# Down weights' sums on GpSimd, last norms and flips reordered, seven low parts made by accumulating DMAs

## The chip, the cores and the metric

The kernel runs on one core of a Trainium2 chip. Its time is the device time of one launch in microseconds (us). Five engines work side by side, each through its own queue of instructions in order: TensorE (PE, matmuls), VectorE (DVE), ScalarE (ACT), GpSimd (POOL) and SyncE (SP, which issues the loads here). DMAs run beside them. Engines wait for each other by semaphores.

## What is computed

One layer of a decoder trunk for 512 tokens of width 1024, in float32: attention with forget gates, a projection and a norm, a gated MLP with a short causal convolution (2816 channels), a second norm, and an embedding that is projected and gated into the result.

```python
mix = fox_mixer(x, attn_w_in, attn_b_f, attn_w_out)
x = layer_norm(ALPHA * x + mix, ln_mix_g, ln_mix_b)
u, g = jnp.split(x @ ffn_w_up, [FFN_DIM], axis=-1)
g = causal_dwconv(g, ffn_conv_w, ffn_conv_b)
ffn = (jax.nn.gelu(g, approximate=False) * u) @ ffn_w_down
x = layer_norm(ALPHA * x + ffn, ln_ffn_g, ln_ffn_b)
gate = jax.nn.sigmoid(x @ ple_w_gate + ple_b_gate)
out = x + gate * (p @ ple_w_proj)
```

## The kernel before

**Every product is three matmuls.** A float32 operand is cut into a high part (rounded to fp32r) and a low part (the rest); hi x hi, hi x lo and lo x hi are added in PSUM (`three`, L107).

**Weights arrive in units of 128 x 1024** (class `Weights`): a load from HBM into one of 4 `raw` buffers, ACT copies it to `whi` (L85), DVE takes `wlo = raw - whi` (L86), each into one of 5 buffers. `get(i, ahead)` hands out unit i and has the units up to i + ahead cut before it, so that the cutting instructions of the units ahead stand in the queues before the work on unit i.

**The stages** are: the input projections and attention (16 heads), with the output projection begun among the last heads; the norm of the mixer (L492, L494: two instructions for each 512 columns of a tile of 128 tokens); `up` with 22 pairs of gate and value tiles; `down` in two parts, behind 6 and behind 5 pairs of channel blocks; the second norm; the embedding product `pl` (L107, PSUM tiles `pl`); the gates `gt`; the output.

**`down` is a Strassen-Winograd product.** The halves of tokens, of channels and of output columns make blocks; seven block products replace eight. Four groups of units are worked one behind the other: `ua` (plain), `ub` (t12: two sums for a unit, L157 and L158, the second into the buffer `side`), `uc` (t3: one sum, L165), `ud` (t4: one sum with `side`, L172, of half size). The sums are over 128 x 512 weights, 4 for each of the 11 pairs, 44 in all, on DVE. The products go to six PSUM banks: x, y and z, two each. When a group ends, DVE adds its banks into the residual `y` (`give`, `add_half`, L476 and L478), and the next group's matmuls into that bank wait for it.

**The tail.** Behind part 1's `uc` the tiles of tokens 2 and 3 are complete, and `half_stats` and `norm` (L483 to L494, with one tiny POOL instruction, the power, L489) run for them; `ud` completes the tiles 0 and 1 one behind the other. `flip` (L502 to L507) transposes a normed tile on PE (`nt`), and ACT and DVE cut it into `x2h` and `x2l`, from which the gates are computed. The embedding products are seven of six matmuls and the four flips stand among them.

**The order** of each engine's instructions is made when the program is built: the scheduler keeps the code's order in the main, and lets an instruction pass another where its own cost figures say that it is ready earlier. So the code's order and each queue's differ by a few places. POOL does little but the attention's rescaling (L357, 64 instructions) and the eight powers.

Of the kernel before, what the change touches and what calls it, by code (L numbers as in the profile page):

```python
# [8 lines left out]
F32 = mybir.dt.float32  # L9
# [38 lines left out]
class Weights:  # L48
# [7 lines left out]

    def add(self, src, n=UNIT, inner=None, make=None):

        self.units.append((src, n, inner, make))
        return len(self.units) - 1  # L60

    def load_to(self, i):
        while self.loaded < min(i, len(self.units)):
            src, n, inner, make = self.units[self.loaded]
            t = self.pool.tile([P, UNIT], F32, tag="raw", name=f"raw{self.loaded}", bufs=RAW_BUFS)
            v = t[:, :n]
            if inner is not None:
                v = v.rearrange("p (a b) -> p a b", b=inner)
            self.nc.sync.dma_start(v, src)
            if make is not None:  # L70
                make(None)
            self.raw[self.loaded] = t
            self.loaded += 1

    def cut_to(self, i):
        while self.cut < min(i, len(self.units)):
            self.load_to(self.cut + 1)
            _, n, _, make = self.units[self.cut]
            t = self.raw.pop(self.cut)
# [3 lines left out]
            for piece in [t[:, :n]] if make is None else make(t):  # L83
                e = c + piece.shape[-1]
                self.nc.scalar.activation(hi[:, c:e], piece, AF.Copy)  # L85
                self.nc.vector.tensor_sub(lo[:, c:e], piece, hi[:, c:e].bitcast(F32))  # L86
                c = e
# [10 lines left out]
def trunk_layer(ctx: ExitStack, tc: tile.TileContext, xT, x2d, pT, wqk, wv0, wv1, wv2, bf, wo, wup, cwb,  # L98
# [46 lines left out]
    def down_units(part):  # L145
# [3 lines left out]
        def t12(j, i):  # L149
            def make(t):  # L150
# [5 lines left out]
                t1, t2 = t[:, :512], side[part][:, i, :]  # L156
                nc.vector.tensor_sub(t1, t1, t2)  # L157
                nc.vector.tensor_sub(t2, t[:, 512:], t1)  # L158
                return [t1, t2]
            return make  # L160

        def t3(t):
            if t is None:
                return None
            nc.vector.tensor_sub(t[:, :512], t[:, 512:], t[:, :512])  # L165
            return [t]

        def t4(i):
            def make(t):
                if t is None:  # L170
                    return None
                nc.vector.tensor_sub(t[:, :512], t[:, :512], side[part][:, i, :])  # L172
                return [t[:, :512]]
            return make
# [9 lines left out]
    for part in range(2):  # L184
        for f in range(2 * PAIRS[part][0], 2 * PAIRS[part][-1] + 2):
            u_up.append([W.add(wup[f, s], inner=P) for s in (1, 0)])
        u_dn.append(down_units(part))
    u_p = W.add(pT.rearrange("(k p) t -> p k t", p=P), inner=S)
    u_pl = [W.add(half_rows(wpl, 0, 2, n), inner=512) for n in range(2)]
    u_g = [[W.add(half_rows(wg, 2 * j, 2, n), inner=512) for j in range(4)] for n in range(2)]  # L190

# [293 lines left out]
    def norm(t, g, b):  # L485
# [3 lines left out]
        nc.gpsimd.tensor_tensor(mv[:, 3:4], mv[:, 2:3], neghalf, op=ALU.pow)  # L489
        for n in range(2):  # L490
            c = slice(n * 512, (n + 1) * 512)
            nc.vector.scalar_tensor_tensor(y[:, t, c], y[:, t, c], mv[:, 0:1], g[:, c],  # L492
                                           op0=ALU.subtract, op1=ALU.mult)
            nc.vector.scalar_tensor_tensor(y[:, t, c], y[:, t, c], mv[:, 3:4], b[:, c],  # L494
                                           op0=ALU.mult, op1=ALU.add)

# [76 lines left out]
    def down(part, hh, hl):  # L573
# [4 lines left out]
        A11, A22, A12, S1, S2, S3, S4 = range(7)  # L578
        acc = {(b, i): bank(f"{b}{part}{i}") for b in "xyz" for i in range(2)}
        seen, opened = set(), set()  # L580

        def step(b, i, a, u, col, first, last):

            j, u = u
            hi, lo = W.get(u)
            c, tk = slice(col * 512, col * 512 + 512), slice(a * HALF + i * P, a * HALF + (i + 1) * P)
# [4 lines left out]

        def chain(b, a, us, col, n):
            for i in range(2):
                step(b, i, a, us[n], col, n == 0, n == len(us) - 1)

# [26 lines left out]
        give("z", 0, 1)  # L622
        if part == 1:
            for t in (2, 3):
                for n in range(2):
                    half_stats(t, n)
                norm(t, g2, b2)
        us = list(enumerate(ud))
        for i in range(2):
            for n in range(len(js)):  # L630
                step("x", i, A22, us[n], 0, n == 0, n == len(js) - 1)
            give1("x", 1, 0, i)
            if part == 1:
                for n in range(2):
                    half_stats(i, n)
                norm(i, g2, b2)
                if i == 1:
                    flip(2, x2h, x2l)

# [33 lines left out]
    pl = base.tile([P, NT, D], F32, tag="xl", name="pl")  # L673
    W.cut_to(u_p + 3)

    def embed(ps, up, ul, p0, pw, lo_c=0, w=512):

        ph, plo = W.parts[up]
        hi, lo = W.get(ul)
        for k in range(2):  # L680
# [4 lines left out]
    for i, (n, t) in enumerate([(n, t) for n in range(2) for t in tiles][:-1]):  # L685
        ps = bank(f"pl{t}_{n}")
        embed(ps, u_p, u_pl[n], t * P, S)
        nc.scalar.activation(pl[:, t, n * 512:(n + 1) * 512], ps, AF.Copy)
        if i in (1, 3, 6):
            flip({1: 3, 3: 0, 6: 1}[i], x2h, x2l)  # L690

# [23 lines left out]
    for n in range(2):  # L715
        for t in tiles[:NT - n]:
            finish(n, t, gate(n, t), pl[:, t, n * 512:(n + 1) * 512])
    tz = tiles[-1]
# [53 lines left out]
```

## Time and profile before

| what | value |
|---|---|
| median of three runs | 677.21 us (676.69 to 678.17) |
| the profiled execution | 679.51 us |
| its span, first to last instruction | 677.8 us |
| mean granted TensorE clock | 0.986 |
| loads from HBM | 76.26 MB |

The trace is of one execution. A busy share is an average over stages, and where an engine is nearly always busy, what can be won lies in the few places where it is not. Those are found in three steps: the busy tenths over 40 slices of the span show where, the view of waits names which instruction waited and for whom, and the view of windows gives PE's busy time and granted clock in a stretch. The clock matters, since a matmul at a lower clock counts as busy all the same.

### The profile page before, as it was taken

The page shows a single profiled execution, that of the slowest core. Times are in us where ns is not written, and L with a number is a line of the kernel's source. Part 1 is how long each engine was busy: PE and PEld are TensorE (multiplying, and loading weights), DVE is VectorE, ACT ScalarE, POOL GpSimd, SP SyncE. Part 2 cuts the span into 40 slices and gives each one's busy share as a digit, 9 for nine tenths or more (in the row PEclk, how much of TensorE's full clock was granted, in tenths as well). Part 3 has the DMA queues.
Part 4 walks back from the last instruction along what each step waited for, and adds up shares of the span by engine and source line. Part 5 has one row for each costly group of instructions (what it writes and reads, how often), then busy time and mean ns, then how long its engine had stood idle before and what let it go on. Part 6 is the DMA issues. An engine that isn't in the chain of part 4 may idle for free.

```text
span 677.8 us, 8719 instructions
## 1 busy us (share of the span) xinstructions
PE 657.6 (97%) x3222; PEld 556.8 (82%) x3222; DVE 477.5 (70%) x762; ACT 314.9 (46%) x517; POOL 80.9 (12%) x78
## 2 busy tenths in 40 slices
PE   8999999999999999999999998999999999986997
PEld 7899888888888889888888886888888888765886
DVE  6664799999984895565556597565555669898454
ACT  5644687777774144344344343154344435243331
POOL 0000555544452110000000000000000000010000
PEclk9999999999999999999999998999999999996999
DMA  8533211221181314332233354572233327454321
GB/s 282 156 126 125 62 65 64 64 61 39 61 301 57 110 63 137 102 104 93 94 94 93 112 170 138 180 255 94 93 100 91 99 85 247 141 155 122 103 79 46
DMA packets 34011, 79.06 MB, mean 117 GB/s; under 512 B 3056, under 2 KB 6896, under 8 KB 33968
## 3 DMA queue, kind: packets, MB, share of 16 engines
q1 hardware_dynamic: 33968, 78.50, 36.0%
q8 instruction: 25, 0.41, 0.2%
q14 instruction: 18, 0.15, 0.1%
HBM read 76.26 MB, written 2.10 MB: 116 GB/s over the span
## 4 chain that ended last, share of the span: by engine, by line
PE 82%; DVE 8%; DMA 5%; issue 2%; ACT 2%; SPq 0%; ACTq 0%; DVEq 0%
PE g L107 17%; PE u L107 17%; PE pp L107 12%; PE gt L107 6%; PE pv L107 5%; PE x L107 5%; DMA raw<-wdn 4%; PE ao L107 3%; PE o L383 3%; DVE wlo L86 2%; PE t L370 2%; PE ap L107 2%; PE z L107 2%; PE pl L107 2%; PE s L339 1%
## 5 line engine op out<-in xcount | busy, mean ns | idle before, releaser
L86 DVE TENSOR_TENSOR wlo<-raw,whi 128x1024 fp32r<-128x1024 f32 (+4 forms) x138 | 149.4, 1089 | 80.2 <-ACT whi L85 79.7
L85 ACT ACTIVATE whi<-raw 128x1024 fp32r<-128x1024 f32 (+4 forms) x138 | 131.5, 956 | 158.1 <-PE g L107 51.9
L357 POOL TENSOR_SCALAR pr<-pr,rl 128x128 f32<-128x128 f32 (+1 forms) x64 | 72.8, 1157 | 134.9 <-DVE rl L353 132.7
L107 PE MATMUL g<-x1l,whi 128*128 128x512 f32 (+1 forms) x192 | 71.4, 372 | 1.2 <-DVE x1l L507 1.2
L107 PE MATMUL g<-x1h,whi 128*128 128x512 f32 (+1 forms) x192 | 71.4, 372 | 0.0
L107 PE MATMUL g<-x1h,wlo 128*128 128x512 f32 (+1 forms) x192 | 71.3, 371 | 0.0
L107 PE MATMUL u<-x1l,whi 128*128 128x512 f32 (+1 forms) x184 | 69.9, 380 | 0.0
L107 PE MATMUL u<-x1h,whi 128*128 128x512 f32 (+1 forms) x184 | 69.9, 380 | 0.0
L107 PE MATMUL u<-x1h,wlo 128*128 128x512 f32 (+1 forms) x184 | 69.9, 380 | 0.0
L489 POOL TENSOR_TENSOR mv<-mv,neghalf 128x1 f32<-128x1 f32 x8 | 7.3, 913 | 397.9 <-DVE mv L488 375.6
L107 PE MATMUL pp<-xh,wlo 128*128 128x512 f32 x128 | 50.2, 392 | 0.0
L107 PE MATMUL pp<-xl,whi 128*128 128x512 f32 x128 | 50.0, 391 | 0.0
L107 PE MATMUL pp<-xh,whi 128*128 128x512 f32 x128 | 49.9, 390 | 0.0
L107 PEld LDWEIGHTS g<-x1l,whi 128*128 128x128 f32 x192 | 36.2, 188 | 7.7 <-DVE x1l L507 1.4
L349 ACT ACTIVATE pr<-s,nm 128x128 f32<-128x128 f32 (+1 forms) x64 | 33.5, 526 | 16.8 <-DVE nm L348 15.8
L107 PEld LDWEIGHTS g<-x1h,wlo 128*128 128x128 f32 x192 | 36.2, 188 | 6.2
L107 PEld LDWEIGHTS g<-x1h,whi 128*128 128x128 f32 x192 | 36.1, 188 | 6.2
L107 PEld LDWEIGHTS u<-x1h,wlo 128*128 128x128 f32 x184 | 34.6, 188 | 6.6
L107 PEld LDWEIGHTS u<-x1h,whi 128*128 128x128 f32 x184 | 34.6, 188 | 6.5
L107 PEld LDWEIGHTS u<-x1l,whi 128*128 128x128 f32 x184 | 34.6, 188 | 6.5
L557 DVE TENSOR_TENSOR E<-a,u 128x512 f32<-128x512 f32 x22 | 15.1, 688 | 34.2 <-PE u L107 32.7
L556 ACT ACTIVATE a<-a 128x512 f32<-128x512 f32 x22 | 13.9, 632 | 52.6 <-DVE a L554 52.6
(156 smaller groups left out, 1430.5 us busy)
## 6 DMA issues: line engine op xcount, KB each, us to landing
raw<-wup SPq DMA_DIRECT2D x44, 512.0 KB
raw<-wdn SPq DMA_DIRECT2D x33, 512.0 KB
raw<-wqk SPq DMA_DIRECT2D x16, 512.0 KB
raw<-wo SPq DMA_DIRECT2D x8, 512.0 KB
raw<-wg SPq DMA_DIRECT2D x8, 512.0 KB
raw<-wv SPq DMA_DIRECT2D x8, 384.0 KB
side<-wdn SPq DMA_DIRECT2D x11, 256.0 KB
raw<-wdn SPq DMA_DIRECT2D x11, 256.0 KB
```

What stands on the lines that cost most here:

```text
L85: self.nc.scalar.activation(hi[:, c:e], piece, AF.Copy)
L86: self.nc.vector.tensor_sub(lo[:, c:e], piece, hi[:, c:e].bitcast(F32))
L107: nc.tensor.matmul(ps, lhsT, rhs, start=start and n == 0, stop=stop and n == 2, skip_group_check=on)
L339: nc.tensor.matmul(ps[:, :n], QA[:, q], KA[:, :n], start=True, stop=False)
L349: nc.scalar.activation(pr[:, off:off + w], ps[:, :w], AF.Exp, bias=nm[:, i:i + 1], accum_out=ls[:, i:i + 1])
L357: nc.gpsimd.tensor_scalar_mul(pr[:, off:off + w], pr[:, off:off + w], rl[:, i:i + 1])
L370: nc.tensor.transpose(ps[:, w:w + P], pr[:, o:o + P], ident)
L383: nc.tensor.matmul(ps[:, q0:], V[:, j, h], p[:, o:o + w], start=j == 0 and n == 0, stop=j == NT - 1 and n == 1)
L489: nc.gpsimd.tensor_tensor(mv[:, 3:4], mv[:, 2:3], neghalf, op=ALU.pow)
L556: nc.scalar.activation(a, a, AF.Gelu)
L557: nc.vector.tensor_mul(e, a, pu)
```

## The change

Six things are done at once.

- The 44 sums of the down weights are issued to GpSimd instead of DVE.
- Seven units (`pT`, the two of the embedding weights `wpl`, the first four of the gate weights `wg`) get their low part in another way (`by_dma`): ACT writes the negative of the weights, rounded to fp32r like `whi`, into `wlo` (L88 after), and a DMA that POOL issues adds the float32 weights from HBM to it (L90 after).
- A norm's two steps take 1024 columns in one instruction each instead of 512 in two (8 norms).
- `get` cuts 2 units ahead in the groups `ua`, `ub` and `uc`, and 3 in `ud` and in the embedding, instead of 1; the fixed cut of the three embedding units goes.
- In `ud` the loop runs over units outside and over the two banks inside. The norms of tiles 2 and 3 stand behind the matmuls of `ud`, those of tiles 0 and 1 behind the first gate.
- The flips: tile 2 behind the embedding products, tile 3 behind the first gate, then 0 and 1 each a gate later. The banks are allotted in the order y, z, x.

```diff
--- before.py
+++ after.py
@@ -54,14 +54,15 @@
         self.units, self.raw, self.parts = [], {}, {}
         self.loaded = self.cut = 0
 
-    def add(self, src, n=UNIT, inner=None, make=None):
-
-        self.units.append((src, n, inner, make))
+    def add(self, src, n=UNIT, inner=None, make=None, by_dma=False):
+
+
+        self.units.append((src, n, inner, make, by_dma))
         return len(self.units) - 1
 
     def load_to(self, i):
         while self.loaded < min(i, len(self.units)):
-            src, n, inner, make = self.units[self.loaded]
+            src, n, inner, make, _ = self.units[self.loaded]
             t = self.pool.tile([P, UNIT], F32, tag="raw", name=f"raw{self.loaded}", bufs=RAW_BUFS)
             v = t[:, :n]
             if inner is not None:
@@ -75,7 +76,7 @@
     def cut_to(self, i):
         while self.cut < min(i, len(self.units)):
             self.load_to(self.cut + 1)
-            _, n, _, make = self.units[self.cut]
+            src, n, inner, make, by_dma = self.units[self.cut]
             t = self.raw.pop(self.cut)
             hi = self.pool.tile([P, UNIT], F32R, tag="whi", name=f"whi{self.cut}", bufs=SPLIT_BUFS)
             lo = self.pool.tile([P, UNIT], F32R, tag="wlo", name=f"wlo{self.cut}", bufs=SPLIT_BUFS)
@@ -83,7 +84,12 @@
             for piece in [t[:, :n]] if make is None else make(t):
                 e = c + piece.shape[-1]
                 self.nc.scalar.activation(hi[:, c:e], piece, AF.Copy)
-                self.nc.vector.tensor_sub(lo[:, c:e], piece, hi[:, c:e].bitcast(F32))
+                if by_dma:
+                    self.nc.scalar.activation(lo[:, c:e], piece, AF.Copy, scale=-1.0)
+                    v = lo[:, :n].rearrange("p (a b) -> p a b", b=inner)
+                    self.nc.gpsimd.dma_start(v, src, accum_op=ALU.add)
+                else:
+                    self.nc.vector.tensor_sub(lo[:, c:e], piece, hi[:, c:e].bitcast(F32))
                 c = e
             self.parts[self.cut] = (hi, lo)
             self.cut += 1
@@ -154,22 +160,22 @@
                     nc.sync.dma_start(side[part][:, i, :], wdn[2 * j * P:(2 * j + 1) * P, 0:512])
                     return None
                 t1, t2 = t[:, :512], side[part][:, i, :]
-                nc.vector.tensor_sub(t1, t1, t2)
-                nc.vector.tensor_sub(t2, t[:, 512:], t1)
+                nc.gpsimd.tensor_sub(t1, t1, t2)
+                nc.gpsimd.tensor_sub(t2, t[:, 512:], t1)
                 return [t1, t2]
             return make
 
         def t3(t):
             if t is None:
                 return None
-            nc.vector.tensor_sub(t[:, :512], t[:, 512:], t[:, :512])
+            nc.gpsimd.tensor_sub(t[:, :512], t[:, 512:], t[:, :512])
             return [t]
 
         def t4(i):
             def make(t):
                 if t is None:
                     return None
-                nc.vector.tensor_sub(t[:, :512], t[:, :512], side[part][:, i, :])
+                nc.gpsimd.tensor_sub(t[:, :512], t[:, :512], side[part][:, i, :])
                 return [t[:, :512]]
             return make
 
@@ -185,9 +191,10 @@
         for f in range(2 * PAIRS[part][0], 2 * PAIRS[part][-1] + 2):
             u_up.append([W.add(wup[f, s], inner=P) for s in (1, 0)])
         u_dn.append(down_units(part))
-    u_p = W.add(pT.rearrange("(k p) t -> p k t", p=P), inner=S)
-    u_pl = [W.add(half_rows(wpl, 0, 2, n), inner=512) for n in range(2)]
-    u_g = [[W.add(half_rows(wg, 2 * j, 2, n), inner=512) for j in range(4)] for n in range(2)]
+    u_p = W.add(pT.rearrange("(k p) t -> p k t", p=P), inner=S, by_dma=True)
+    u_pl = [W.add(half_rows(wpl, 0, 2, n), inner=512, by_dma=True) for n in range(2)]
+    u_g = [[W.add(half_rows(wg, 2 * j, 2, n), inner=512, by_dma=n == 0) for j in range(4)]
+           for n in range(2)]
 
     tiles = (2, 3, 0, 1)
     tl = slice(tiles[-1] * P, tiles[-1] * P + P)
@@ -487,12 +494,8 @@
         nc.vector.bn_aggr(mv[:, 0:2], stats.pop(t))
         nc.vector.tensor_scalar_add(mv[:, 2:3], mv[:, 1:2], EPS)
         nc.gpsimd.tensor_tensor(mv[:, 3:4], mv[:, 2:3], neghalf, op=ALU.pow)
-        for n in range(2):
-            c = slice(n * 512, (n + 1) * 512)
-            nc.vector.scalar_tensor_tensor(y[:, t, c], y[:, t, c], mv[:, 0:1], g[:, c],
-                                           op0=ALU.subtract, op1=ALU.mult)
-            nc.vector.scalar_tensor_tensor(y[:, t, c], y[:, t, c], mv[:, 3:4], b[:, c],
-                                           op0=ALU.mult, op1=ALU.add)
+        nc.vector.scalar_tensor_tensor(y[:, t], y[:, t], mv[:, 0:1], g, op0=ALU.subtract, op1=ALU.mult)
+        nc.vector.scalar_tensor_tensor(y[:, t], y[:, t], mv[:, 3:4], b, op0=ALU.mult, op1=ALU.add)
 
     def flip(t, xh, xl):
 
@@ -576,22 +579,22 @@
         js = PAIRS[part]
         ua, ub, uc, ud = u_dn[part]
         A11, A22, A12, S1, S2, S3, S4 = range(7)
-        acc = {(b, i): bank(f"{b}{part}{i}") for b in "xyz" for i in range(2)}
+        acc = {(b, i): bank(f"{b}{part}{i}") for b in "yzx" for i in range(2)}
         seen, opened = set(), set()
 
-        def step(b, i, a, u, col, first, last):
+        def step(b, i, a, u, col, first, last, ahead=2):
 
             j, u = u
-            hi, lo = W.get(u)
+            hi, lo = W.get(u, ahead)
             c, tk = slice(col * 512, col * 512 + 512), slice(a * HALF + i * P, a * HALF + (i + 1) * P)
             three(acc[b, i], hi[:, c], lo[:, c], hh[:, j, tk], hl[:, j, tk],
                   first and (b, i) not in opened, last, weights_move=True, on=(b, i) in opened)
             if last:
                 opened.add((b, i))
 
-        def chain(b, a, us, col, n):
+        def chain(b, a, us, col, n, ahead=2):
             for i in range(2):
-                step(b, i, a, us[n], col, n == 0, n == len(us) - 1)
+                step(b, i, a, us[n], col, n == 0, n == len(us) - 1, ahead)
 
         def give(b, half, n):
             for i in range(2):
@@ -620,22 +623,15 @@
             chain("z", S4, us, 1, n)
         give("x", 1, 1)
         give("z", 0, 1)
-        if part == 1:
-            for t in (2, 3):
-                for n in range(2):
-                    half_stats(t, n)
-                norm(t, g2, b2)
         us = list(enumerate(ud))
+        for n in range(len(js)):
+            chain("x", A22, us, 0, n, 3)
+        for t in (2, 3) if part == 1 else ():
+            for n in range(2):
+                half_stats(t, n)
+            norm(t, g2, b2)
         for i in range(2):
-            for n in range(len(js)):
-                step("x", i, A22, us[n], 0, n == 0, n == len(js) - 1)
             give1("x", 1, 0, i)
-            if part == 1:
-                for n in range(2):
-                    half_stats(i, n)
-                norm(i, g2, b2)
-                if i == 1:
-                    flip(2, x2h, x2l)
 
     flip(2, x1h, x1l)
     g2 = b2 = x2h = x2l = None
@@ -671,12 +667,11 @@
 
 
     pl = base.tile([P, NT, D], F32, tag="xl", name="pl")
-    W.cut_to(u_p + 3)
 
     def embed(ps, up, ul, p0, pw, lo_c=0, w=512):
 
         ph, plo = W.parts[up]
-        hi, lo = W.get(ul)
+        hi, lo = W.get(ul, 3)
         for k in range(2):
             c = slice(k * 512 + lo_c, k * 512 + lo_c + w)
             pk = slice(k * pw + p0, k * pw + p0 + P)
@@ -686,8 +681,7 @@
         ps = bank(f"pl{t}_{n}")
         embed(ps, u_p, u_pl[n], t * P, S)
         nc.scalar.activation(pl[:, t, n * 512:(n + 1) * 512], ps, AF.Copy)
-        if i in (1, 3, 6):
-            flip({1: 3, 3: 0, 6: 1}[i], x2h, x2l)
+    flip(2, x2h, x2l)
 
 
     bgs = row(hpool.tile([P, D], F32, tag="hl", name="bgs"), bg)
@@ -714,7 +708,16 @@
 
     for n in range(2):
         for t in tiles[:NT - n]:
-            finish(n, t, gate(n, t), pl[:, t, n * 512:(n + 1) * 512])
+            e = gate(n, t)
+            if n == 0 and t == 2:
+                flip(3, x2h, x2l)
+                for o in range(2):
+                    for c in range(2):
+                        half_stats(o, c)
+                    norm(o, g2, b2)
+            elif n == 0 and t != 1:
+                flip({3: 0, 0: 1}[t], x2h, x2l)
+            finish(n, t, e, pl[:, t, n * 512:(n + 1) * 512])
     tz = tiles[-1]
     es = [gate(1, tz, c, 256) for c in (0, 256)]
     for e, c in zip(es, (0, 256)):
```

Three places show what this does to the queues. The line numbers of the rows below are those of each program: L86 before is L92 after, L165 is L171, L476 and L478 are L483 and L485, L489 is L496, L492 and L494 are L497 and L498, L507 is L510.

**DVE in part 0, at the turn from `ub` to `uc`**, before. The sums (L165) are those of `uc`'s units, the wlo (L86) theirs, and L476 is the half that frees a bank (`z` or `x`):

```order
L165 TENSOR_TENSOR raw_3824<-raw_3824 128x512
L86 TENSOR_TENSOR wlo_3862<-raw_3802,whi_3861 128x1024
L165 TENSOR_TENSOR raw_3843<-raw_3843 128x512
L86 TENSOR_TENSOR wlo_3881<-raw_3824,whi_3880 128x1024
L165 TENSOR_TENSOR raw_3866<-raw_3866 128x512
L165 TENSOR_TENSOR raw_3885<-raw_3885 128x512
L476 SCALAR_TENSOR_TENSOR y<-y,z_3609 128x512
L86 TENSOR_TENSOR wlo_3900<-raw_3843,whi_3899 128x1024
L476 SCALAR_TENSOR_TENSOR y<-y,x_3605 128x512
L476 SCALAR_TENSOR_TENSOR y<-y,x_3606 128x512
L476 SCALAR_TENSOR_TENSOR y<-y,z_3610 128x512
```

The same place after:

```order
L92 TENSOR_TENSOR wlo_3819<-raw_3760,whi_3818 128x1024
L92 TENSOR_TENSOR wlo_3838<-raw_3782,whi_3837 128x1024
L92 TENSOR_TENSOR wlo_3861<-raw_3804,whi_3860 128x1024
L483 SCALAR_TENSOR_TENSOR y<-y,z_3599 128x512
L92 TENSOR_TENSOR wlo_3880<-raw_3823,whi_3879 128x1024
L483 SCALAR_TENSOR_TENSOR y<-y,x_3601 128x512
L483 SCALAR_TENSOR_TENSOR y<-y,x_3602 128x512
L483 SCALAR_TENSOR_TENSOR y<-y,z_3600 128x512
L92 TENSOR_TENSOR wlo_3899<-raw_3842,whi_3898 128x1024
```

The sums have left the queue. Ahead of the first half of z now stand the low parts of `uc`'s units 0, 1 and 2 (wlo_3819 to wlo_3861), and ahead of the halves of x that of unit 3 (wlo_3880).

**POOL at its end**, after. Before, its last instructions are the powers (L489) alone, without a DMA. L178 is the last sum of `ud`, L90 the accumulating DMAs, L496 the powers of the last norms:

```order
L178 TENSOR_TENSOR raw_5081<-raw_5081,side_4790 128x512
L90 DMA wlo_5133<-pT 128x2x512
L496 TENSOR_TENSOR mv<-mv,neghalf 128x1 x2
L90 DMA wlo_5146<-wpl 128x2x512
L90 DMA wlo_5159<-wpl 128x2x512
L90 DMA wlo_5194<-wg 128x2x512
L90 DMA wlo_5199<-wg 128x2x512
L496 TENSOR_TENSOR mv<-mv,neghalf 128x1 x2
L90 DMA wlo_5240<-wg 128x2x512
L90 DMA wlo_5299<-wg 128x2x512
```

The powers of the tiles 2 and 3 stand behind the DMA of `pT`, those of the tiles 0 and 1 behind the DMAs of the first two gate units.

**ACT in the tail**, after (L86 the high parts, L88 the negatives, L683 the embedding's copies from PSUM, L509 the flips' high parts):

```order
L683 ACTIVATE pl<-pl_0_5222 128x512
L86 ACTIVATE whi_5239<-raw_5163 128x1024
L683 ACTIVATE pl<-pl_0_5230 128x512
L88 ACTIVATE wlo_5240<-raw_5163 128x1024
L683 ACTIVATE pl<-pl_1_5238 128x512
L683 ACTIVATE pl<-pl_1_5253 128x512
L86 ACTIVATE whi_5298<-raw_5203 128x1024
L683 ACTIVATE pl<-pl_1_5261 128x512
L509 ACTIVATE x2h<-nt 128x4x128 x2
L88 ACTIVATE wlo_5299<-raw_5203 128x1024
```

wlo_5240 and wlo_5299 are gate units 2 and 3. The negative of unit 3 stands behind the last copy of the embedding and the two of the first flip. Before, DVE made the low parts of the tail behind its norms:

```order
L492 SCALAR_TENSOR_TENSOR y<-y,mv,g2b_4781 128x512 x2
L494 SCALAR_TENSOR_TENSOR y<-y,mv,g2b_4781 128x512 x2
L86 TENSOR_TENSOR wlo_5226<-raw_5147,whi_5225 128x1024
L86 TENSOR_TENSOR wlo_5230<-raw_5157,whi_5229 128x1024
L507 TENSOR_TENSOR x2l<-nt,x2h 128x4x128 x4
```

The last norm's four instructions stand there ahead of the low parts of both embedding units (wlo_5226, wlo_5230).

## Prediction

> **What bounds the kernel now.** I read the page first: the engines, the busy tenths, the chain that ended last.
>
> ```profile
> PE 657.6 (97%) x3222; PEld 556.8 (82%) x3222; DVE 477.5 (70%) x762; ACT 314.9 (46%) x517; POOL 80.9 (12%) x78
> PE   8999999999999999999999998999999999986997
> PEclk9999999999999999999999998999999999996999
> PE 82%; DVE 8%; DMA 5%; issue 2%; ACT 2%; SPq 0%; ACTq 0%; DVEq 0%
> ```
>
> TensorE (PE) is busy 97% of 677.8 us, and most of the chain is its own work. The change takes no matmul away, so it can only win where PE waits or runs at a lower granted clock. A tenth is lost in slice 25 (from 407 us on), and more in slices 36 to 37 (593 to 627), where the clock too is at its lowest. The view of PE's waits names them, and the view of windows sizes them (columns: length, then PE, PEld, DVE, ACT, POOL busy with instruction counts, granted clock, DMA share, GB/s).
>
> ```profile
> PE nt L502 <- DVE x2l L507: 3.8, 1, 3.8
> PE pl L107 <- DVE wlo L86: 2.5, 1, 2.5
> PE z L107 <- DVE y L476: 2.5, 1, 2.5
> PE z L107 <- DVE y L478: 1.3, 1, 1.3
> PE g L107 <- DVE x1l L507: 1.2, 1, 1.2
> 405.00:425.00 20.00, 16.94 (x61) 13.00 (x61) 15.63 (x21) 6.48 (x7) 0.00 (x0) 0.83 0.45 141
> 578.00:590.00 12.00, 10.66 (x47) 8.26 (x46) 11.02 (x16) 3.39 (x4) 0.00 (x0) 1.00 0.38 117
> 603.00:628.00 25.00, 17.44 (x75) 13.14 (x74) 21.30 (x35) 10.99 (x17) 2.77 (x3) 0.80 0.45 138
> 425.74 1.36 PE x L107 x6
> 627.25 1.03 PE L502 MATMUL nt<-ident,y 128*128 128x128 f32 x8
> ```
>
> At full clock six 512-column matmuls take 1.36 us, 0.227 each, and eight transposes 1.03, 0.13 each. So 405 to 425, with 61 matmuls, holds 61 x 0.227 = 13.8 us of work: **6.2 lost**. 578 to 590: 12 - 47 x 0.227 = **1.3 lost**. 603 to 628, with 75, of which 32 are transposes: 43 x 0.227 + 32 x 0.13 = 13.9, **11.1 lost**. With the 1.2 us before the gates of the convolution, about 20 us lie within reach of this change.
>
> **Part 1: the sums of the down weights.** Part 0's turn from the second to the third group of units, on DVE and PE (start, duration, instruction, and in brackets what it waited for):
>
> ```profile
> 412.50 0.69 DVE L165 TENSOR_TENSOR raw<-raw 128x512 f32<-128x512 f32 x1 [0.89 <-DMA raw<-wdn]
> 414.90 0.69 DVE L165 TENSOR_TENSOR raw<-raw 128x512 f32<-128x512 f32 x1 [1.70 <-DMA raw<-wdn]
> 415.50 0.68 DVE L476 SCALAR_TENSOR_TENSOR y<-y,z 128x512 f32<-128x512 f32 x1
> 417.24 1.28 DVE L476 SCALAR_TENSOR_TENSOR y<-y,x 128x512 f32<-128x512 f32 x2
> 416.33 0.47 PE L107 MATMUL z<-whi,hh 128*128 128x512 f32 x1 [2.50 <-DVE y L476]
> 417.97 0.80 PE L107 MATMUL x<-whi,hh 128*128 128x512 f32 x1 [0.56 <-DVE y L476]
> ```
>
> DVE works in order. The sums of the next units stand ahead of the two halves that free the accumulators (z, then x), and wait for their loads; the halves wait behind them, and PE behind the halves. Then the clock falls: matmuls take 0.47 and 0.80 us. In the changed order the waiting sums are on GpSimd (POOL), but DVE's first half of z now stands behind the low parts (wlo) of the third group's units 0 to 2, and the x halves behind that of unit 3. A wlo waits for its high part (whi) and so for POOL's sum. **So the wait is replaced, not removed**, and its size is set by how long a sum takes on POOL. The nearest rows:
>
> ```profile
> L165 DVE TENSOR_TENSOR raw<-raw 128x512 f32<-128x512 f32 x11 | 7.5, 685 | 3.0 <-DMA raw<-wdn 2.9
> L86 DVE TENSOR_TENSOR wlo<-raw,whi 128x1024 fp32r<-128x1024 f32 x102 | 123.6, 1217 | 63.0 <-ACT whi L85 62.9
> L85 ACT ACTIVATE whi<-raw 128x1024 fp32r<-128x1024 f32 x102 | 107.6, 1059 | 114.7 <-PE g L107 51.9 <-PE u L107 12.9 <-PE x L107 9.7
> L357 POOL TENSOR_SCALAR pr<-pr,rl 128x512 f32<-128x512 f32 x16 | 25.9, 1619 | 0.0
> L357 POOL TENSOR_SCALAR pr<-pr,rl 128x128 f32<-128x128 f32 x16 | 12.4, 772 | 134.9 <-DVE rl L353 132.7 <-DMA side<-wdn 2.2
> 112.51 1.49 POOL L357 TENSOR_SCALAR pr<-pr,rl 128x128 f32<-128x128 f32 x1 [2.60 <-DVE rl L353]
> 112.34 1.18 DVE L86 TENSOR_TENSOR wlo<-raw,whi 128x1024 fp32r<-128x1024 f32 x1
> 384.85 3.84 DMA raw<-wdn
> ```
>
> The same sum takes DVE 0.69. POOL's own work at that size has one tensor input and takes 1.62; for two inputs nothing excludes twice that less its start, 1.619 + (1.619 - 0.772) x 512/384 = 2.75. So the time s of one sum lies between 0.69 and 2.75. I take **1.3**: between DVE's row and POOL's, nearer POOL's.
>
> By the Trainium skill, page GPSIMD Engine Reference, section Performance versus the Vector engine, a two-input add of 2048 elements takes GpSimd 1.96 times DVE's time; with DVE's row that would be an estimate of 1.34 and cost some 0.5 us more in the sum. No row here shows that operation.
>
> There is a second cost. At 112.34 DVE runs a wlo, which has two SBUF inputs; the POOL instruction that starts 0.17 us later takes 1.49 where the group's mean is 0.77. So a sum on POOL stands still beside a wlo, and I add the two instead of laying one beside the other.
>
> The Trainium skill, page SBUF — State Buffer, section Who interferes with whom, has this as a rule that speaks against the change: a DVE instruction with two SBUF inputs and a GpSimd one that reads SBUF take the shared port in turn, and whoever issued first blocks the other for its whole length. The row at 112.51 agrees for POOL; that DVE waits for POOL, no row shows.
>
> The walk: unit 2 of the second group has its raw weights in at 384.85 + 3.84 = 388.7. POOL then does four units of two sums, 2s + 1.2 of wlo each, and four of the third group at s + 1.15: with s = 1.3, 15.2 + 9.8, to 413.7. Then whi 1.06, wlo 1.2 and the first x half 0.64: PE can go on with x at **416.6**, in general at 401.0 + 12s. The z half stands one unit earlier, at about 414. That leaves PE 0.4 + 1.8 = 2.2 us of stall against 3.06; I assume that pauses this short leave the clock up (the 1.3 us pause at 578 to 590 did, clock 1.00), and round the loss to 2.5. Gain 6.2 - 2.5 = **3.7**; should the clock fall all the same, 0.7. At s = 1.1 all 6.2 are gained, at 1.4 nothing (417.8, later than before), at 1.62 it is 420.4, 3 us worse. In part 1 the same walk over five units with s = 1.3 ends at 579, ahead of the stall of before, so **1.3** is gained, up to about s = 1.45.
>
> DVE itself loses 44 x 0.685 = 30 us of sums. I cost that at nothing more, since its last-ending waits are the ones counted here.
>
> **Part 2: norms over 1024.** Two instructions of 512 become one, so each norm saves at most two starts, and the wlo that stands ahead of x1l in the mixer's norm is done earlier; what PE waits for there is the 1.2 us of row g. I take **0.8**, bounds -0.5 (two long instructions keep a short one waiting) and 1.2.
>
> **Part 3: the tail.** The rows of before:
>
> ```profile
> 612.82 1.97 PE L502 MATMUL nt<-ident,y 128*128 128x128 f32 x8 [3.83 <-DVE x2l L507]
> 617.33 0.79 PE L107 MATMUL pl<-wlo,whi 128*128 128x512 f32 x1 [2.54 <-DVE wlo L86]
> 628.04 0.48 PE L107 MATMUL gt<-whi,x2h 128*128 128x512 f32 x1
> 616.06 2.35 DVE L86 TENSOR_TENSOR wlo<-raw,whi 128x1024 fp32r<-128x1024 f32 x2
> 409.91 4.89 DMA raw<-wdn
> ```
>
> DVE runs the norms of all four tiles ahead of the wlo of the embeds, and PE pays 3.8 + 2.5 and a low clock (0.80). Afterwards the embeds (42 matmuls, 9.5 us) follow the down product directly; the norms lie under them, and DVE has no wlo there. In its place ACT writes the negative copy, 1.06 us each, and an accumulating DMA from POOL completes wlo. The trace has no such DMA. From issue to landing it lasts L: at least the 3.8 of a plain 512 KB load (384.85), and 9.8 if it moves everything twice at the slower pace of 4.89. I take **6**, between them.
>
> Let E be PE's end of the down product. A unit's two copies cost ACT 2.1, and a unit's buffer frees with the down unit five before it, so the negatives are ready at E - 3.3 (p), E - 1.2, E + 0.9 (the two embed units), E + 2.9 and E + 5.0 (gate units 0 and 1). With L = 6, p lands at E + 2.7: one matmul is ahead of it, a stall of 2.5; the first embed unit lands at E + 4.8, 0.3 to 0.9 behind need. The embeds end at T = E + 12.7 instead of 9.5: 3.2 lost. Flipping tile 2 then gives PE about 1.5 of waiting for ACT and DVE. Gate unit 3 takes p's buffer, free only at T, so its negative is ready at T + 3.9 behind four other ACT instructions and lands at T + 9.9; PE wants it at T + 7.5: 2.4. The flip of tile 0 ahead of its gate costs 0.5. Together 7.6 of 11.1: gain **3.5**. Each us of L counts about twice: L = 3.8 gains 8.4, L = 9.8 loses 3.5, break-even 7.75.
>
> The buffer order "yzx", the bias load and the last units' place on SP's queue move nothing that PE waits for in these rows, since the raw loads of the tail are in before the copies.
>
> **Sum.** 3.7 + 1.3 + 0.8 + 3.5 = 9.3. The profiled execution took 679.5, so 670.2; it lies 2.3 above the median of the three runs, 677.2, so **668** for the median.
>
> **The rivals.**
> - Partial gain: the x half stands behind four wlo, and the clock falls as before (gain 0.7 instead of 3.7), or L is 8 to 10 and the tail gives nothing. For it: each step in the chain POOL, ACT, DVE, PE is in order. 3 to 7 us less: 671 to 676.
> - Better: L near 4 and s near 1.1. Then 6.2 + 1.3 + 0.8 + 8.4 = 16.7, 660.5. For it: the load of 3.84 moves as many bytes.
> - Slower, by one mechanism: POOL's queue of sums is the bound of the down stages. It decides from s = 1.65: part 0 loses 12 x (1.65 - 1.35) = 3.6, part 1 has no gain left, and that eats the 4.3 of parts 2 and 3. At 2.75 the x half comes at 434.0, 17 later, the units behind it are paced by 3.9 against PE's 2.72 (12 matmuls), and part 1 pays nearly as much: some 30 us, 707. For it: POOL's row of 1.62 and its standing still beside wlo. Against: that row runs another operation, partly beside wlo itself.
> - The change only moves the waits and nothing comes of it: 676 to 678.5.
>
> **Chances.** Forecast (664 to 671) 0.43, partial gain (671 to 675.9) 0.2, better 0.12, about the same 0.07, slower 0.18. A change of 0.2%, 1.35 us, is about what a measurement of this kernel can tell from none. So faster 0.75, same 0.07, slower 0.18. The range leaves out the far end of the better case and most of the slower one: 661 to 680.
>
> **What would show it.** In the profile after: the duration of a sum on POOL (1.3; over 1.65 the sign turns) and whether DVE's wlo grow beside them; PE's waits at z and x in part 0, at most 2.2 in all, with the clock near 1.0 from 405 to 425; the landing of the accumulating DMAs (6 us after issue), and PE's waits at the first embed (2.5) and at gate unit 3 (2.4); from the end of the down product to the first gate matmul some 16 us where it is 25 now. Wrong at once: a wait of PE for POOL or for a whi of the second group, or DVE's halves later than 418.

## The result, and the profile after

The changed kernel takes 703.52 us (701.18 to 703.73, four runs) against 677.36: 1.038 times the kernel before (95% interval 1.035 to 1.040). Forecast were 668.0, range 661 to 680. The profiled execution took 701.18, the fastest of the four, with a span of 699.0. The page of after, and its view of PE's waits:

```profile
PE 661.7 (95%) x3222; PEld 559.9 (80%) x3222; DVE 466.7 (67%) x695; ACT 321.2 (46%) x524; POOL 164.8 (24%) x129
PE   8999999999999999999999899999999999564897
PEclk9999999999999999999999999999999999887999
PE gt L113 <- DVE x2l L510: 6.7, 1, 6.7
PE gt L113 <- DMA wlo<-wg: 6.6, 2, 3.6
PE pl L113 <- DMA wlo<-pT: 5.4, 1, 5.4
PE pl L113 <- DMA wlo<-wpl: 4.7, 1, 4.7
PE x L113 <- DVE y L485: 2.4, 2, 1.6
PE x L113 <- DVE y L483: 2.3, 1, 2.3
PE g L113 <- DVE x1l L510: 0.4, 1, 0.4
```

The dip at slice 25 has gone to slice 23 (from 384 us on), and the one near the end is deep and long: five waits, 23 us together, in the embedding and the first gate. Set side by side by PE's first and last matmul of a stage, in us, in the two profiled executions:

| stage | before | after | change |
|---|---|---|---|
| start to the first matmul of `down`, part 0 | 381.0 | 379.4 | -1.6, 0.85 of it in the mixer's norm |
| `down`, part 0 | 64.0 | 61.6 | -2.4 |
| `down`, part 1 | 49.6 | 50.8 | +1.2 |
| end of `down` to PE's last matmul | 70.5 | 94.5 | **+24.0** |

All of the loss is in the tail. Its windows in after, the embeds, the first two gates, the rest (columns as in the prediction):

```profile
600.00:625.00 25.00, 14.19 (x45) 10.28 (x44) 7.21 (x12) 9.88 (x14) 3.67 (x3) 0.73 0.76 184
625.00:658.00 33.00, 18.66 (x68) 14.06 (x67) 9.58 (x13) 7.36 (x10) 5.69 (x5) 0.79 0.51 103
658.00:695.00 37.00, 36.61 (x196) 31.18 (x193) 21.09 (x31) 11.24 (x17) 0.00 (x0) 1.00 0.15 57
```

Waits and a clock of 0.73 and 0.79 stretch the first two; the third is at full clock and busy. What POOL does there (start, duration; in brackets its idle time and what ended it), and DVE beside it:

```profile
597.11 1.37 POOL L90 DMA_DIRECT2D wlo<-pT  x1 [8.06 <-ACT wlo L88]
598.08 1.51 POOL L496 TENSOR_TENSOR mv<-mv,neghalf 128x1 f32<-128x1 f32 x2
606.20 1.24 POOL L90 DMA_DIRECT2D wlo<-wpl  x1 [6.60 <-issue]
614.72 1.21 POOL L90 DMA_DIRECT2D wlo<-wpl  x1 [7.28 <-issue]
621.39 1.22 POOL L90 DMA_DIRECT2D wlo<-wg  x1 [5.47 <-ACT whi L86]
628.03 1.20 POOL L90 DMA_DIRECT2D wlo<-wg  x1 [5.42 <-ACT x2h L509]
628.78 1.05 POOL L496 TENSOR_TENSOR mv<-mv,neghalf 128x1 f32<-128x1 f32 x1
```

```profile
605.98 0.79 PE L113 MATMUL pl<-whi,wlo 128*128 128x512 f32 x1 [5.36 <-DMA wlo<-pT]
614.50 0.80 PE L113 MATMUL pl<-wlo,whi 128*128 128x512 f32 x1 [4.74 <-DMA wlo<-wpl]
629.87 1.28 DVE L498 SCALAR_TENSOR_TENSOR y<-y,mv,g2b 128x1024 f32<-128x1024 f32 x1 [22.65 <-POOL mv L496]
634.79 0.79 PE L113 MATMUL gt<-whi,x2l 128*128 128x512 f32 x1 [6.71 <-DVE x2l L510]
DMA to landing us min/median/max: 6.1/6.6/8.8
```

The last line is the time from issue to landing of all seven DMAs. PE gets pT's low part at 605.98, and the next DMA is issued at 606.20; it gets wpl's at 614.50, and the next goes at 614.72. ACT had those negatives ready at 598.7 and 600.6. **Only one of these DMAs is under way at a time**, and POOL sits in front of the next (its idle time there ends by "issue", with nothing in the program to wait for). The last powers stand behind five of them; DVE waits 22.65 us for one, has `x2l` behind it in its own queue, and PE waits 6.7 for that.

### The profile page after: what moved, and what is told of

The parts are those of the page before. It is cut to its first block, busy times and chain, and to the rows that moved or that the text cites. A ratio compares the mean times of both kernels' runs of the same rounds, so it can differ in the third digit from the quotient of the medians.

```text
span 699.0 us, 8726 instructions
## 1 busy us (share of the span) xinstructions
PE 661.7 (95%) x3222; PEld 559.9 (80%) x3222; DVE 466.7 (67%) x695; ACT 321.2 (46%) x524; POOL 164.8 (24%) x129
## 4 chain that ended last, share of the span: by engine, by line
PE 86%; DVE 4%; DMA 4%; issue 3%; ACT 2%; POOL 1%; SPq 0%; POOLq 0%; DVEq 0%; ACTq 0%
PE g L113 17%; PE u L113 17%; PE pp L113 12%; PE x L113 7%; PE pv L113 6%; PE gt L113 6%; PE z L113 4%; PE ao L113 3%; PE o L390 3%; PE t L377 2%; PE ap L113 2%; DVE wlo L92 2%; PE y L113 2%; PE s L346 1%; PE s L348 1%
## 5 line engine op out<-in xcount | busy, mean ns | idle before, releaser
L92 DVE TENSOR_TENSOR wlo<-raw,whi 128x1024 fp32r<-128x1024 f32 (+5 forms) x131 | 155.8, 1193 | 87.0 <-ACT whi L86 85.3
L86 ACT ACTIVATE whi<-raw 128x1024 fp32r<-128x1024 f32 (+4 forms) x138 | 131.9, 956 | 159.9 <-PE g L113 54.7
L163 POOL TENSOR_TENSOR raw<-raw,side 128x512 f32<-128x512 f32 x11 | 18.0, 1637 | 244.9 <-DMA raw<-wdn 132.5
L356 ACT ACTIVATE pr<-s,nm 128x128 f32<-128x128 f32 (+1 forms) x64 | 33.4, 525 | 16.9 <-DVE nm L355 15.8
L113 PE MATMUL x<-whi,hh 128*128 128x512 f32 x88 | 34.9, 396 | 4.7 <-DVE y L485 2.4
```

The costliest lines, as they stand in the source:

```text
L113: nc.tensor.matmul(ps, lhsT, rhs, start=start and n == 0, stop=stop and n == 2, skip_group_check=on)
L163: nc.gpsimd.tensor_sub(t1, t1, t2)
L356: nc.scalar.activation(pr[:, off:off + w], ps[:, :w], AF.Exp, bias=nm[:, i:i + 1], accum_out=ls[:, i:i + 1])
```

## Experiments

Ratios are to the kernel before, run beside them (677.8 to 678.0).

### The tail without the accumulating DMAs

```diff
-    u_p = W.add(pT.rearrange("(k p) t -> p k t", p=P), inner=S, by_dma=True)
+    u_p = W.add(pT.rearrange("(k p) t -> p k t", p=P), inner=S)
```

and the same for `wpl` and `wg`.

> The changed kernel with the seven low parts taken by DVE again (no accumulating DMA); sums on POOL and the new order stay. Theory A (the accumulating DMAs run one at a time on POOL's queue, and the powers of the last norms stand between them: that is where the 24 us of the tail went): the tail comes back and the order's own gain shows, 666 to 671 us. Theory B (the new order of norms and flips costs the tail its time, the DMAs only seem to): 690 us or more. Theory C (POOL's sums delay everything, as the slower rival said): 697 us or more.

Measured: **667.64**, 0.985 (0.982 to 0.988). With all the sums on DVE again as well:

```diff
-                nc.gpsimd.tensor_sub(t1, t1, t2)
-                nc.gpsimd.tensor_sub(t2, t[:, 512:], t1)
+                nc.vector.tensor_sub(t1, t1, t2)
+                nc.vector.tensor_sub(t2, t[:, 512:], t1)
...
-            nc.gpsimd.tensor_sub(t[:, :512], t[:, 512:], t[:, :512])
+            nc.vector.tensor_sub(t[:, :512], t[:, 512:], t[:, :512])
...
-                nc.gpsimd.tensor_sub(t[:, :512], t[:, :512], side[part][:, i, :])
+                nc.vector.tensor_sub(t[:, :512], t[:, :512], side[part][:, i, :])
```

> As e1, and the 44 sums on DVE again: the new order, the long norms and the deeper cutting alone. Theory A: 668 to 673 us, with the down parts within 2 us of the kernel before; the difference to e1 is what the sums on POOL are worth, +1 to +4 us. Theory B: 690 us or more. Theory C: some 20 us below e1.

Measured: 667.49, 0.985 (0.983 to 0.987), just under the 668 to 673 expected. Theory A holds, B and C fall. The embeds of e1, in a window:

```profile
600.50:610.30 9.80, 9.80 (x45) 8.05 (x44) 9.80 (x13) 5.54 (x10) 2.78 (x2) 1.00 0.65 225
```

PE is busy throughout, at full clock. The new order (with the deeper cutting, which no run parts from it) is worth some 10 us in the tail: from the end of `down` to PE's last matmul 60.6 us in e1 and 60.5 in e3, 70.5 before. The DMAs cost 36 us, 34 of them in the tail's 94.5. But the sums on POOL are worth nothing in all, where 1 to 4 us were expected.

### Why one at a time

The program sets the space for the descriptors of POOL's DMAs (the entries that say what is to be moved). Here it is doubled:

```diff
-    nc = bacc.Bacc("TRN2", target_bir_lowering=False, num_devices=1, dynamic_dma_scratch_size=1024)
+    nc = bacc.Bacc("TRN2", target_bir_lowering=False, num_devices=1, dynamic_dma_scratch_size=2048)
```

> The changed kernel, with twice the space for the descriptors of POOL's DMAs (2048 instead of 1024 bytes a partition), nothing else. Theory A1 (that space holds one of these DMAs, so the next is issued when the one before has landed): two run at a time, wpl's first is issued about 2 us after pT's instead of 9, and the time falls to 682 to 688 us. Theory A2 (accumulating DMAs go one at a time whatever the space): 703 us, issues still 0.3 us behind landings.

Measured: **684.74**, 1.010 (1.007 to 1.013). And with 4096:

> As r2048 with space for four. Theory A1: four run at a time; what is left is the landing of the first (5.4 us of PE's wait at the first embed) and gate unit 3 (2 to 3 us), 677 to 683 us; if they share a pace when side by side, each lands later than 8.8 us after its issue. Theory A2: 703 us.

Measured: 684.63, 1.010 (1.007 to 1.012). POOL's rows, first with 2048, then with 4096, and for the latter the time to landing of the first DMA and of the fifth:

```profile
600.66 1.37 POOL L90 DMA_DIRECT2D wlo<-pT  x1 [8.54 <-ACT wlo L88]
602.68 2.94 POOL L90 DMA_DIRECT2D wlo<-wpl  x2
610.52 1.22 POOL L90 DMA_DIRECT2D wlo<-wg  x1 [4.89 <-issue]
```

```profile
596.23 1.37 POOL L90 DMA_DIRECT2D wlo<-pT  x1 [8.05 <-ACT wlo L88]
598.25 2.94 POOL L90 DMA_DIRECT2D wlo<-wpl  x2
601.88 1.19 POOL L90 DMA_DIRECT2D wlo<-wg  x1 [0.69 <-ACT wlo L88]
604.32 1.19 POOL L90 DMA_DIRECT2D wlo<-wg  x1 [1.24 <-ACT wlo L88]
DMA to landing us min/median/max: 9.1/9.1/9.1
DMA to landing us min/median/max: 17.7/17.7/17.7
```

The space is why they go one at a time (A1). With 2048 three go at once, not two, and the fourth waits for the first landing (600.66 + 9.6 = 610.3); with 4096 none waits for another. That is worth 18 of the 34 us of the tail, which takes 76.3 with 2048. Yet the second doubling wins nothing, against the expectation of 677 to 683: the five then land at 605.3 to 622.0, (622.0 - 605.3) / 4 = **4.2 us apart**. Side by side they share a pace, a whole unit each 4.2 us, so that the fifth lands 17.7 after its issue. The first takes 9.1 (8.8 in the changed kernel, where it is alone), and PE still waits 5.6 for it.

To see what the accumulation itself does, the same DMAs without it (`wlo` then holds the weights, so this kernel leaves the seven low parts out):

```diff
-                    self.nc.gpsimd.dma_start(v, src, accum_op=ALU.add)
+                    self.nc.gpsimd.dma_start(v, src)
```

> The changed kernel, its seven DMAs of POOL without the accumulation: they copy the weights into wlo, rounded, so these low parts are left out (wlo holds the weights). Same queue, same bytes from HBM, same space. Theory A1 (space for the descriptors of one): issues still 0.3 us behind the landing before. Theory A2 (accumulating is what makes them go one at a time): several at a time, 685 us or less. How long one lasts from issue to landing, against 6.1 to 8.8, shows what the accumulation itself costs: the same if the queue's pace is the limit, 4 to 5 us if reading the destination is.

Measured: 679.42, 1.001 (1.000 to 1.003). Its rows, with the time to landing of the first and of the fifth:

```profile
602.56 0.93 POOL L90 DMA_DIRECT2D wlo<-pT  x1 [7.96 <-ACT wlo L88]
604.56 0.73 POOL L90 DMA_DIRECT2D wlo<-wpl  x1
606.33 0.72 POOL L90 DMA_DIRECT2D wlo<-wpl  x1 [1.03 <-ACT wlo L88]
610.32 0.72 POOL L90 DMA_DIRECT2D wlo<-wg  x1 [3.27 <-issue]
614.17 0.71 POOL L90 DMA_DIRECT2D wlo<-wg  x1 [3.13 <-issue]
DMA to landing us min/median/max: 7.4/7.4/7.4
DMA to landing us min/median/max: 8.0/8.0/8.0
```

Three copies fit into the space that holds one accumulating DMA, and the fourth goes 0.3 us behind the first landing (602.56 + 7.4 = 610.0). So the queue blocks for any DMA when its space is full, and an accumulating one takes more of it: its issue lasts 1.2 us instead of 0.72. Landings are (614.2 + 8.0 - 610.0) / 4 = 3.1 us apart. With 2048, where three accumulating DMAs are under way as three copies are here, they are (615.1 + 11.7 - 610.3) / 4 = 4.1 apart, so accumulating also makes each a third slower. Something of both A1 and A2 is there: they go one at a time because of the space, not because of the addition, but the addition is why the space holds only one.

Halves of the DMA, the space as it was:

```diff
-                    self.nc.gpsimd.dma_start(v, src, accum_op=ALU.add)
+                    for k in range(2):
+                        self.nc.gpsimd.dma_start(v[:, k], src[:, k], accum_op=ALU.add)
```

> The changed kernel with each accumulating DMA in two of half the size (256 KB), space unchanged at 1024 bytes. Theory A1 (the space is counted in descriptors): two halves are under way together, the second issued 1 us behind the first, a third only when one has landed; a unit is complete about as early as before or somewhat earlier, 692 to 702 us. Rival A3 (one accumulating DMA at a time at this space, whatever its size): each half is issued 0.3 us behind the landing of the one before, 14 landings one behind the other, later than 703 us.

Measured: 687.09, 1.013 (1.009 to 1.017), better than A1 expected; A3 falls. Issues at 602.15, 602.94 and 604.54, the fourth at 608.85 behind the first landing at 608.6: three halves fit. All four counts agree if an accumulating DMA takes twice the space of a copy, and 1024 bytes hold three units of a copy's space but not four. That reading is inferred from the counts.

### Which of the units cost what

```diff
-    u_g = [[W.add(half_rows(wg, 2 * j, 2, n), inner=512, by_dma=n == 0) for j in range(4)]
+    u_g = [[W.add(half_rows(wg, 2 * j, 2, n), inner=512, by_dma=False) for j in range(4)]
```

> The changed kernel with accumulating DMAs for the three units of the embedding only; the four gate units' low parts on DVE. Theory A: the embeds still last 24 to 25 us from the end of the down product (their waits of 5.4 and 4.7 stay), the last powers stand behind three DMAs instead of five, PE's waits for x2l (6.7) and for the gates' wlo (6.6) go; 683 to 689 us. Theory D (any of these DMAs on POOL holds the powers up, and that is the main cost): above 695 us.

Measured: 681.88, 1.006 (1.004 to 1.009), 1 us under the expected range. Embeds 24.7 us, then gates as without DMAs. The other half of them:

```diff
-    u_p = W.add(pT.rearrange("(k p) t -> p k t", p=P), inner=S, by_dma=True)
-    u_pl = [W.add(half_rows(wpl, 0, 2, n), inner=512, by_dma=True) for n in range(2)]
+    u_p = W.add(pT.rearrange("(k p) t -> p k t", p=P), inner=S)
+    u_pl = [W.add(half_rows(wpl, 0, 2, n), inner=512) for n in range(2)]
```

> The counterpart: accumulating DMAs for the four gate units only, the embedding's low parts on DVE. Theory A: the embeds last 10 us as without these DMAs, the powers come early, and the first gate waits for its units, 6.5 us apart: 10 to 15 us of waits; 677 to 684 us. The costs of p3 and p4 over the version without DMAs (667.6) together come near the 36 us of all seven, or fall short by what both overlap.

Measured: 684.72, 1.010 (1.007 to 1.013). Embeds 9.7 us. PE's waits in it:

```profile
PE gt L113 <- DVE x2l L510: 10.0, 1, 10.0
PE gt L113 <- DMA wlo<-wg: 1.3, 1, 1.3
```

Most of its cost is not the gates' own data, 1.3 us: the powers stand behind the DMAs here too, and PE waits 10 us for `x2l`. The expectation had the powers early and was wrong in that; the time is 0.7 above its range. In the tails alone p3 costs 15.0 us and p4 13.8 over e1, all seven 33.9: together they cost 5 us more than apart.

### The sums

e1 with the two sums of t12 on DVE, those of t3 and t4 left on POOL:

```diff
-                nc.gpsimd.tensor_sub(t1, t1, t2)
-                nc.gpsimd.tensor_sub(t2, t[:, 512:], t1)
+                nc.vector.tensor_sub(t1, t1, t2)
+                nc.vector.tensor_sub(t2, t[:, 512:], t1)
```

> Without accumulating DMAs, the two sums of the second group on DVE, those of the third and fourth on POOL. Theory E (what a sum on POOL holds up is the wlo that DVE has ahead of a freeing half: at the turn into the second group with two sums on POOL, 4.0 + 2.1 us of waits at x; at the turn into the third with the sum on DVE, 3.0 + 1.7 at z): each turn has its better engine, and both stalls shrink: 661 to 665 us. Theory F (DVE's order alone makes these stalls, whichever engine sums): 667 us, waits at x or z of 4 us or more.

Measured: **663.31**, 0.979 (0.977 to 0.981): 2.1% less than the kernel before. The counterpart, e1 with the other two lines of e3's diff:

> The counterpart of the version at 663.3: the two sums of the second group on POOL, those of the third and fourth on DVE, no accumulating DMAs. Theory E: both turns have their worse engine, PE waits at x at the turn into the second group (4 + 2 us) and at z at the turn into the third (3 + 1.7): 669 to 673 us. Theory F (the engine of the sums does not matter, the version at 663.3 had another order by chance): 665 to 667 us.

Measured: 671.53, 0.991 (0.989 to 0.992), in the range of theory E. But the waits at z that it named did not come: PE waits at x (4.3 and 2.4 us), and its view of waits has none at z. The four versions without accumulating DMAs:

| | second group's sums on POOL | on DVE |
|---|---|---|
| third and fourth group's on POOL | 667.64 (e1) | **663.31** (b1) |
| on DVE | 671.53 (b2) | 667.49 (e3) |

By the times, moving the second group's sums to POOL costs 4.3 and 4.0 us, moving the others gains 3.9 and 4.2. PE's waits bear out two of these steps. From e3 to b1 the waits at z fall from 3.0 and 1.7 us to 0.6 and 0.2; from b1 to e1 those at x grow from 0.7 and 1.3 to 4.0 and 2.1. So e1 and e3 come to the same time with a stall at another turn each. The 3.9 between b2 and e1 is something else. `down` in two parts, in e1 and then in b2:

```profile
379.00:442.00 63.00, 58.99 (x254) 48.30 (x253) 47.59 (x46) 24.53 (x31) 35.87 (x22) 0.97 0.52 166
550.60:600.90 50.30, 48.24 (x212) 39.42 (x212) 43.49 (x48) 21.37 (x26) 25.39 (x16) 1.00 0.54 171
379.80:444.40 64.60, 60.27 (x254) 49.09 (x253) 53.00 (x59) 25.23 (x31) 15.88 (x10) 0.95 0.51 163
553.10:605.50 52.40, 49.96 (x212) 40.57 (x211) 46.70 (x58) 21.24 (x26) 9.49 (x6) 0.97 0.52 165
```

For the same matmuls PE is busy 3.0 us longer in b2, at a lower clock; its waits at x are only 0.6 longer. That the clock falls further because of the last sums is not shown: it differs so between versions with the same sums too (see the end). What those sums cost on DVE is shown by e3 against b1 alone.

DVE in e1, ahead of the turn into the second group, POOL beside it, and what PE pays:

```profile
391.56 1.78 DVE L92 TENSOR_TENSOR wlo<-raw,whi 128x512 fp32r<-128x512 f32 x1
393.26 1.78 DVE L92 TENSOR_TENSOR wlo<-side,whi 128x512 fp32r<-128x512 f32 x1
398.33 1.75 DVE L92 TENSOR_TENSOR wlo<-raw,whi 128x512 fp32r<-128x512 f32 x1
400.00 1.27 DVE L483 SCALAR_TENSOR_TENSOR y<-y,x 128x512 f32<-128x512 f32 x2
402.39 0.68 DVE L92 TENSOR_TENSOR wlo<-side,whi 128x512 fp32r<-128x512 f32 x1
391.05 1.74 POOL L163 TENSOR_TENSOR raw<-raw,side 128x512 f32<-128x512 f32 x1
392.87 1.62 POOL L164 TENSOR_TENSOR side<-raw 128x512 f32<-128x512 f32 x1
401.16 1.28 POOL L171 TENSOR_TENSOR raw<-raw 128x512 f32<-128x512 f32 x1
400.82 0.77 PE L113 MATMUL x<-whi,hh 128*128 128x512 f32 x1 [4.01 <-DVE y L483]
```

A wlo that takes DVE 0.68 alone takes 1.78 beside POOL's sums, and a sum of 1.28 takes 1.62 to 1.74: they go in turn, DVE 1.1 us behind each sum. Seven wlo in a row lose 7.7 us so, with the freeing halves of x (400.00) behind them, and PE stalls 4.0. In b1 what is left at these turns:

```profile
PE x L113 <- DVE y L485: 1.3, 1, 1.3
PE x L113 <- DVE y L483: 0.7, 1, 0.7
PE z L113 <- DVE y L483: 0.6, 1, 0.6
```

### The long norms

The kernel before with this edit alone, and then b1 with it undone:

```diff
-        for n in range(2):
-            c = slice(n * 512, (n + 1) * 512)
-            nc.vector.scalar_tensor_tensor(y[:, t, c], y[:, t, c], mv[:, 0:1], g[:, c],
-                                           op0=ALU.subtract, op1=ALU.mult)
...
+        nc.vector.scalar_tensor_tensor(y[:, t], y[:, t], mv[:, 0:1], g, op0=ALU.subtract, op1=ALU.mult)
```

> The kernel before with the norms' long instructions alone (part 2 of the prediction), nothing else of the change. By the prediction: 0.8 us less in the mixer's norm; in the tail DVE saves some starts: 675 to 677 us, with PE's wait for x1l at 0.4. Rival: the 9 to 10 us that the tail wins without the DMAs come from the long norms and not from the order: 667 to 669 us.

Measured: 676.29, 1.000 (0.998 to 1.001), with PE waiting 0.4 us for `x1l`: no difference that can be told, and no sign of the rival's 9 to 10 us.

> The version with the first sums on DVE and no accumulating DMAs (663.3), its norms in halves of 512 again. If the long norms are worth the 0.8 us of the prediction and the order hides the norms of the tail: 664 to 665 us. Rival: the tail's gain needs the long norms: 668 us or more.

Measured: 664.20, 0.980 (0.979 to 0.982); PE's wait for `x1l` is 1.2 us again where b1 has 0.4. The 0.8 us of the prediction is there; the tail's gain does not need the long norms.

## Why the prediction was wrong

**The time of a sum on POOL** was right: 1.28 us undisturbed (forecast 1.3). By the Trainium skill, page GPSIMD Engine Reference, section Performance versus the Vector engine, the estimate was 1.34; the rows agree within 5%. Beside DVE's wlo the means of the four groups of sums are 1.54 to 1.85 us; the prediction had that waiting too, as a term of its own, and forecast that PE can go on with x at 416.6; it goes on at 416.9, without a wait. The slower rival, POOL's queue of sums as the bound from 1.65 us on, did not come: `down` is 1.2 us shorter in all.

**The turn into the third group** went as forecast or better: no stall of PE in part 0 from 402 to 422, and 0.8 us in part 1. What the step missed stands one turn earlier: the halves of x behind the wlo of the second group (2.3 us in part 0, 1.6 in part 1). Behind the 2.3 the clock fell, which the prediction assumed it would not for pauses this short: a matmul there takes 0.63 us instead of 0.39. Gains of 3.7 and 1.3 became 2.4 and -1.2. The prediction laid sums and wlo one behind the other to find when POOL is done; it did not ask what stands behind DVE's wlo while DVE waits for POOL. The rule of the page SBUF — State Buffer (the Trainium skill, section Who interferes with whom) holds in both directions: DVE waits for POOL too, 1.1 us for each wlo that meets a sum.

**The long norms**: 0.8 forecast, 0.8 measured.

**The tail** is the step that failed: forecast a gain of 3.5, measured a loss of 24.0. pT's DMA was issued at E - 3.3, as worked out. Its length was short in the sum: L = 6, measured 6.1 to 8.8, and 8.8 and 8.3 for the first two, for which PE waits; that is over the sum's own break-even of 7.75. The larger error is another: the negatives, ready at E - 1.2, E + 0.9, E + 2.9 and E + 5.0, were taken to land one L later each. That let five DMAs run beside each other, each as long as if alone; only one could. The first embed unit landed at E + 14 instead of E + 4.8, the gates' at E + 27 and later. And the powers, which the order shows behind the DMAs, were given no price: a DMA's issue was taken for a step that never waits. The rival "L is 8 to 10" asked for the length of one, and none asked how many fit. Nor would more space have saved the step: with 2048 a DMA takes up to 14.4 us from issue to landing, and the tail is still 5.8 us longer than before. Of the DMAs' 33.9 us in the tail, 18.1 go with the space; the other 15.8 (their shared pace, the first landing, the clock that falls in PE's waits) are not parted further.

With that step taken out, the same change without its DMAs takes 667.6, near the 668.0 of the forecast, but by luck, since the terms are others: the tail wins 9.9 instead of 3.5, and `down` 0.3 instead of 5.0.

## What to carry to other kernels

- Ahead of issuing several DMAs from POOL, find out how many of them its queue holds. Here a full queue blocked the engine, and with it every small instruction behind the DMA in program order.
- Where two engines stretch each other's instructions, as POOL and DVE do here, what counts is not only the work that is moved, but what stands in order behind the other engine's stretched instructions. A move that pays at one place can cost as much at another; moved by halves, both can be read (663.3 against 667.6).
- A stall that a change takes away at one place and one that it adds at another can cancel, as in e1 and e3. The time of the whole does not show that; the waits by place do.

## What was not expected of the hardware

- An accumulating DMA of 512 KB took 6.1 to 8.8 us alone. With several under way, 4.2 us passed from one landing to the next; with copies through the same queue 3.1.
- Versions with the second group's sums on POOL differ in `down` with the same instructions there: part 0 takes 61.1 to 65.1 us, part 1 49.8 to 52.6. In b1 and its version with short norms, with these sums on DVE, part 0 takes 59.2 in both. The clock has a large part in it. In p4 PE waits 6.8 us at x, in e1 6.1, but the clock is 0.95 and 0.97 in the two parts, where e1 has 0.97 and 1.00, and they take 1.9 and 2.2 us longer. In r4096 PE's matmuls take 0.39 us behind a stall of 3.4, in the changed kernel 0.63 behind one of 2.3. So the length of a stall alone does not say whether the clock falls; what does is open. Executions of one version differ by 4 us too (e1: 665.89 to 670.30), so a difference of that size between two profiled executions says little without a wait that explains it.
